# First feed-forward stage of an encoder layer: a second pair of features by seven products, plain blocks saved unscaled, and two steps exchanged

## The chip, the cores and the metric

The kernel runs on one core of a Trainium2 chip. A core has a matrix engine (TensorE; PE in the profile, its weight loads PEld), three engines for elementwise work (VectorE = DVE, ScalarE = ACT, GpSimd = POOL), a queue engine (SyncE = SP) and 16 DMA engines that bring data from device memory. The metric is the device time of one execution in microseconds, lower is better. The time before is 1250.46 us, the median of three runs that lie between 1250.18 and 1250.67.

## What is computed

One encoder layer on 512 tokens of width 1024: a half-step gated feed-forward network, a mixer of two attention branches, a second half-step feed-forward network, a final norm. The change lies in the two feed-forward stages, which are the same computation with different weights:

```python
def rmsnorm(x, g):
    y = xf * lax.rsqrt(jnp.mean(xf * xf, axis=-1, keepdims=True) + EPS)
    return (y * g.astype(jnp.float32)).astype(x.dtype)

def swiglu(x, w1, w3, w2):
    return (jax.nn.silu(x @ w1) * (x @ w3)) @ w2
...
x = x + 0.5 * swiglu(rmsnorm(x, ffn1_norm[l]), ffn1_w1[l], ffn1_w3[l], ffn1_w2[l])
h = rmsnorm(x, mix_norm[l])
x = x + hybrid_mixer(h, ...)
x = x + 0.5 * swiglu(rmsnorm(x, ffn2_norm[l]), ffn2_w1[l], ffn2_w3[l], ffn2_w2[l])
return rmsnorm(x, final_norm)
```

The hidden width is 2816, which the kernel treats as 22 features of 128 rows each; a feature needs one block of w1 and one of w3 (each 128 columns of weights over K = 1024, 512 KB).

## The kernel before

Activations are held transposed: model dimension on the partitions (eight tiles of 128), the 512 tokens along the free axis. Every float32 product is made of three passes on TensorE: operands are split into a high part H (a rounded copy, made by ACT) and a low part L (the remainder, made by DVE), and `mm3` (L256) adds H·H, H·L and L·H into one PSUM bank.

**Weights.** `self.order` lists all weight blocks of the program in the order of use; `loads` (L192) issues their DMAs as soon as a raw buffer is free, `prep` (L228) splits a raw block into `wh` and `wl` (lines L243 on ACT and L244 on DVE), `weights` (L248) hands the next one to TensorE. Split blocks have three buffers `wh` and one more, `whx`, for every fourth; raw blocks lie in rings `wr`, `wa`, `ws`, `wt`. `turn_of` (L122) orders the DMAs. TensorE's instructions keep the order in which the program writes them. The order on the other engines and on the queues is set ahead of time by a planner, which takes instructions in program order where it can and lets a later one go first when the earlier is not ready by its own estimate. Each queue then works strictly in its order.

**Plain features.** `feat` (L268) multiplies one block of 128 features with all 512 tokens: eight k-tiles of three matmuls of 512 columns, 24 matmuls for a block and 96 for two features. The first two blocks of the program are woven by `pair` (L278), since they run while x still arrives. `done1` and `done3` (L488 to L495) scale a block by `R`, the inverse root mean square of each token, apply SiLU, multiply, and split the result (`keep`). R itself comes from the squares of x (`norm_sq`, L402, hooked at step 12), their column sums on TensorE (`stat_r`, L419, hooked at 23), a power on POOL (L417), and four transposes on TensorE with a copy by ACT (`stat_R`, L428, hooked at 28). Until R is there the first blocks are held in their PSUM banks (the list `held`).

**Pairs by seven products.** The other features go two at a time through `strassen` (L310): seven steps A11, S1, S2, A12, S3, S4, A22 in place of eight, each one weight block of 24 matmuls of 256 columns. A11, A12 and A22 use quarters of the weights as they are; S1 and S3 are sums of two quarters, of which the first is loaded by SP (L224) and the second added onto it by an accumulating DMA of POOL (L225); S2 and S4 are sums made by DVE (L242). The steps S1, S2 and A22 multiply sums of activations, `TH` and `TL`, which `t_steps` (L341) prepares: eight scaled copies by ACT (L353), sums by DVE (L366, L367), splits (L358, L359), and for S3 and S4 new right halves of `hH` and `hL` (`part1`, L361, which may be written only when the plain blocks are done). The products of one pair collect in three PSUM banks: A11, S2, S3 and A22 in one after another ("A"), S1 and S4 in "Y", A12 in "X"; `evict` (L504) takes out the bank after each step. `slots` (L131) interleaves pairs so that steps of different pairs alternate; with `ahead`, used for the first group of stage "b" alone, its first five steps are A11 and A12 of the first pair, A11 of the second, S1 and S2 of the first.

**Stages.** `GROUPS` (L22) gives the plain features and the ends of the groups: in the first feed-forward stage ("a") features 0 to 3 are plain and 4 to 7 make two pairs of the first group, in the second ("b") there are no plain ones. After a group, `blocks` multiplies its features with w2 and adds the result to x.

## Time and profile before

| what | value |
|---|---|
| median of three runs | 1250.46 us |
| time of the profiled execution | 1250.19 us |
| its span in the profile | 1248.4 us |
| granted TensorE clock over the span | 0.998 |
| TensorE busy | 1234.5 us |
| DVE busy | 908.1 us |
| ACT busy | 603.5 us |
| POOL busy | 126.5 us |

The profiled execution ends 1.8 us after its span and lies 0.27 us under the median. A timeline row gives start and duration in us, the engine, the line of the kernel, the operation, and what it writes and reads; in brackets stands the idle time of the engine ahead of it and what ended it. Matmuls are pipelined, so that the distance from one start to the next, not the duration, tells their pace.

### The profile page before, as it was taken

Reading aid. Unit: us, or ns where it says so; the run is one execution under the profiler, and the core shown is the slowest. Engines: PE = TensorE matmul, PEld = TensorE weight load, DVE = VectorE, ACT = ScalarE, POOL = GpSimd, SP = SyncE. Lnnn points to the kernel's source line nnn. Section 1 sums busy time; section 2 is a strip of 40 time slices with the busy share of each in tenths; the row PEclk is TensorE's granted clock in tenths of the full one; section 3 lists DMA queues with packets and bytes.
Section 4 is the critical chain, followed back from the end, with each engine's and each line's share of the span. In section 5 each row is a group of like instructions: output and inputs, shape, how many; then the busy total and the mean of one; then the engine's idle time right before and its main releaser. Section 6 shows DMA issues by size and latency. Waiting matters only on the chain.

```text
span 1248.4 us, 20502 instructions
## 1 busy us (share of the span) xinstructions
PE 1234.5 (99%) x8220; PEld 1115.5 (89%) x8220; DVE 908.1 (73%) x1373; ACT 603.5 (48%) x897; POOL 126.5 (10%) x132
## 2 busy tenths in 40 slices
PE   9999999999999999999999999999999999999997
PEld 7897999899899999978888878888899989988997
DVE  7784688468787887477755898865978747874874
ACT  8551355245464444454423446654565425532553
POOL 1111101000222110200000200000211001100001
PEclk9999999999999999999999999999999999999999
DMA  8875777241488982653343131167767536743222
GB/s 296 230 192 166 195 196 192 95 119 51 143 214 252 233 223 105 226 170 79 94 132 101 51 110 43 66 217 246 205 169 193 163 101 185 187 152 104 66 85 68
DMA packets 90656, 190.85 MB, mean 153 GB/s; under 512 B 12849, under 2 KB 19393, under 8 KB 90561
## 3 DMA queue, kind: packets, MB, share of 16 engines
q1 hardware_dynamic: 71344, 145.46, 34.8%
q0 software_dynamic: 18496, 43.54, 17.4%
q8 instruction: 64, 1.05, 0.4%
q10 hardware_dynamic: 720, 0.55, 0.1%
q14 instruction: 32, 0.25, 0.1%
HBM read 175.79 MB, written 17.38 MB: 155 GB/s over the span
## 4 chain that ended last, share of the span: by engine, by line
PE 94%; DVE 3%; issue 1%; ACT 1%; POOL 0%; DMA 0%; SPq 0%; POOLq 0%; DVEq 0%
PE mm L258 24%; PE mm L260 23%; PE mm L259 23%; PE Y L260 4%; PE Y L259 4%; PE Y L258 4%; PE X L259 2%; PE X L260 2%; PE X L258 2%; PE mm L979 1%; PE S L903 1%; PE Tb L1115 1%; PE T L990 1%; DVE wl L244 0%; PE Sb L260 0%
## 5 line engine op out<-in xcount | busy, mean ns | idle before, releaser
L243 ACT CAST wh<-wr 128x1024 fp32r<-128x1024 f32 x133 | 139.4, 1049 | 188.0 <-PE mm L259 124.0
L244 DVE TENSOR_TENSOR wl<-wr,wh 128x1024 fp32r<-128x1024 f32 x133 | 163.1, 1226 | 55.4 <-ACT wh L243 55.2
L258 PE MATMUL mm<-hH,wh 128*128 128x256 f32 (+1 forms) x560 | 179.8, 321 | 1.7 <-ACT c L514 1.5
L260 PE MATMUL mm<-hH,wl 128*128 128x256 f32 (+1 forms) x560 | 177.2, 316 | 0.9 <-DVE wl L244 0.9
L259 PE MATMUL mm<-hL,wh 128*128 128x256 f32 (+1 forms) x560 | 177.3, 317 | 0.2 <-DVE hL L400 0.2
L258 PE MATMUL mm<-gg,wh 128*128 128x512 f32 (+1 forms) x440 | 166.4, 378 | 0.0
L259 PE MATMUL mm<-gg,wh 128*128 128x512 f32 (+1 forms) x440 | 165.9, 377 | 0.0
L260 PE MATMUL mm<-gg,wl 128*128 128x512 f32 (+1 forms) x440 | 165.9, 377 | 0.0
L258 PEld LDWEIGHTS mm<-hH,wh 128*128 128x128 f32 x560 | 105.4, 188 | 11.0 <-ACT c L514 1.7
L260 PEld LDWEIGHTS mm<-hH,wl 128*128 128x128 f32 x560 | 105.3, 188 | 9.1 <-DVE wl L244 1.3
L259 PEld LDWEIGHTS mm<-hL,wh 128*128 128x128 f32 x560 | 105.5, 188 | 8.3 <-DVE hL L400 1.2
L243 ACT CAST wh<-wa 128x1024 fp32r<-128x1024 f32 x54 | 56.8, 1051 | 97.0 <-PE Y L259 47.1
L258 PEld LDWEIGHTS mm<-gg,wh 128*128 128x128 f32 x440 | 82.6, 188 | 16.6 <-PE mm L260 0.9
L260 PEld LDWEIGHTS mm<-gg,wl 128*128 128x128 f32 x440 | 82.6, 188 | 15.4
L259 PEld LDWEIGHTS mm<-gg,wh 128*128 128x128 f32 x440 | 82.6, 188 | 14.9
L243 ACT CAST wh<-ws 128x1024 fp32r<-128x1024 f32 x54 | 56.8, 1052 | 72.9 <-PE mm L259 51.4
L243 ACT CAST wh<-wt 128x1024 fp32r<-128x1024 f32 x54 | 56.8, 1052 | 67.7 <-PE mm L259 44.0
L258 PE MATMUL mm<-TH,wh 128*128 128x256 f32 x320 | 88.4, 276 | 0.0
L260 PE MATMUL mm<-TH,wl 128*128 128x256 f32 x320 | 88.3, 276 | 0.0
L259 PE MATMUL mm<-TL,wh 128*128 128x256 f32 x320 | 88.3, 276 | 0.0
L244 DVE TENSOR_TENSOR wl<-wt,wh 128x1024 fp32r<-128x1024 f32 x54 | 66.0, 1223 | 30.7 <-ACT wh L243 29.9
L244 DVE TENSOR_TENSOR wl<-wa,wh 128x1024 fp32r<-128x1024 f32 x54 | 66.0, 1221 | 25.2 <-ACT wh L243 25.1
(275 smaller groups left out, 3200.5 us busy)
## 6 DMA issues: line engine op xcount, KB each, us to landing
wr<-in_w2a SPq DMA_DIRECT2D x22, 512.0 KB, 3.3
wt<-in_w13b SPq DMA_DIRECT2D x22, 512.0 KB, 4.2
wa<-in_w13b SPq DMA_DIRECT2D x22, 512.0 KB, 3.6
wt<-in_w13b POOLq DMA_DIRECT2D x22, 512.0 KB, 5.9
wr<-in_w2b SPq DMA_DIRECT2D x22, 512.0 KB, 3.6
wt<-in_w13a SPq DMA_DIRECT2D x18, 512.0 KB, 3.4
wt<-in_w13a POOLq DMA_DIRECT2D x18, 512.0 KB, 6.3
wa<-in_w13a SPq DMA_DIRECT2D x18, 512.0 KB, 3.3
```

The source lines that it names most:

```text
L243: self.nc.scalar.copy(H, raw)
L244: self.nc.vector.tensor_sub(L, raw, f32(H))
L258: mm(out, lH, rH, start=start, stop=False, skip_group_check=more)
L259: mm(out, lH, rL, start=False, stop=False, skip_group_check=more)
L260: mm(out, lL, rH, start=False, stop=stop, skip_group_check=more)
L903: nc.tensor.matmul(*args, start=True, stop=True)
L979: nc.tensor.matmul(oc, v, p, start=st, stop=sp)
L990: nc.tensor.transpose(ps[:, 128 * b:128 * b + 128], P[h][:, c0 + 128 * b:c0 + 128 * b + 128], self.ident)
L1115: nc.tensor.transpose(pt[:, 128 * j:128 * j + 128], P[h, j][:, 128 * k:128 * k + 128], self.ident)
```

## The change

In the first feed-forward stage two features are plain instead of four, and the first group has three pairs instead of two. The four plain blocks are copied out of PSUM by ACT as they are (`save`), and scaled, passed through SiLU, multiplied and split from there (`finish`) after the sixth and the seventh step of the pairs. `stat_r` and `stat_R` move behind the third and the fifth step of the pairs, the squares to step 24 of the plain part, and the preparation of the activation sums starts at step 13 and goes on at every step, with the sum for A22 left for the third step of the pairs. The accumulating DMAs are put into a list, `sums`; those of the first group of stage "a" are written into the program when at most five blocks lie between the block and the one in use. The first loads of the sums in that group have a turn that is one later. `slots` with `ahead` is used for the first group of both stages, and its sixth and seventh step (S3 of the first pair, S1 of the second) change places. Everything behind the first group keeps its form; the indices of the weight blocks behind it grow by three, since eight plain blocks become four and fourteen steps become twenty-one.

```diff
@@ -19,7 +19,8 @@
 BUFS = {"wr": 3, "wa": 3, "ws": 2, "wt": 4, "wh": 3, "whx": 1}
 BASE = {"wh": 160, "whx": 32}
 EARLY, EARLIER = 4, 6
-GROUPS = {"a": (4, 8, 16, 22), "b": (0, 8, 16, 22)}
+NEAR = 5
+GROUPS = {"a": (2, 8, 16, 22), "b": (0, 8, 16, 22)}
 PAIRS = ((0, 0), (1, 0), (0, 1), (0, 2), (1, 1), (1, 2), (2, 0), (3, 0), (2, 1), (2, 2), (3, 1), (3, 2))
 NSQ, FG, FV = 10, 10, 12
 HEAD_G = 4
@@ -112,6 +113,7 @@
             self.order += [(name, m * n + i) for i in range(m)]
         self.order += [(name, i) for name in ("wpb", "wo") for i in range(8)]
         self.order += self.ffn_order("b")
+        self.sums = []
         self.raws, self.tiles, self.used, self.wx, self.TQ, self.stage = {}, [], 0, None, None, None
         self.cap = len(self.order)
         self.rings = {k: [] for k in BUFS}
@@ -125,21 +127,21 @@
         s, f = self.order[n][0][2], self.order[n][1][0]
         if s == "q":
             return max(n - EARLY, self.index["swq", (0, "A11")] - 1)
-        return n - (EARLIER if f >= GROUPS[s][1] else EARLY)
+        return n - (EARLIER if f >= GROUPS[s][1] else EARLY - (s == "a"))
 
     @staticmethod
     def slots(fs, ahead=False):
         at = {7 * i + 2 * j: (f, step) for i, f in enumerate(fs) for j, step in enumerate(STEPS)}
         order = [at[k] for k in sorted(at)]
         if ahead:
-            order[:5] = [order[n] for n in (0, 3, 4, 1, 2)]
+            order[:7] = [order[n] for n in (0, 3, 4, 1, 2, 6, 5)]
         return order
 
     def ffn_order(self, s):
         first, *ends = GROUPS[s]
         items, lo, n = [("w13" + s, i) for i in range(2 * first)], first, 0
         for hi in ends:
-            items += [("sw" + s, at) for at in self.slots(range(lo, hi, 2), not lo)]
+            items += [("sw" + s, at) for at in self.slots(range(lo, hi, 2), lo == first)]
             nf = hi - (0 if n == 0 else lo)
             items += [("w2" + s, n + i) for i in range(nf)]
             n, lo = n + nf, hi
@@ -192,6 +194,8 @@
     def loads(self):
         while self.todo and self.load(self.todo[0]):
             self.todo.pop(0)
+        while self.sums and (not self.sums[0][1] or self.sums[0][0] - self.used <= NEAR):
+            self.sums.pop(0)[2]()
 
     def load(self, n):
         tag = self.kind[n]
@@ -222,7 +226,8 @@
             nc.sync.dma_start(dst, part(step))
         elif tag == "wt":
             nc.sync.dma_start(dst, part("A21"))
-            nc.gpsimd.dma_start(dst, part("A22" if step == "S1" else "A11"), accum_op=ALU.add)
+            self.sums.append((n, name == "sw" + "a" and f < GROUPS["a"][1],
+                              lambda: nc.gpsimd.dma_start(dst, part("A22" if step == "S1" else "A11"), accum_op=ALU.add)))
         return True
 
     def prep(self):
@@ -308,7 +313,7 @@
                     yield from part(c, j)
 
     def strassen(self, s, fs, evict):
-        st, order = {}, self.slots(fs, s == "b" and not fs[0])
+        st, order = {}, self.slots(fs, s != "q" and fs[0] == GROUPS[s][0])
         end = self.used + len(order) - 1
         for f, step in order:
             self.cap = end if f == fs[-1] and step in ("A12", "S3") else len(self.order)
@@ -366,8 +371,8 @@
         sub = lambda o, a, b: nc.vector.tensor_sub(raw[o], raw[a], raw[b])
         neg = lambda o, a, b: nc.vector.scalar_tensor_tensor(raw[o], raw[a], -1.0, raw[b], op0=ALU.mult, op1=ALU.subtract)
         return ([lambda d=d: put(d) for d in range(NK)]
-                + [lambda: sub(0, 0, 1), lambda: sub(1, 3, 1), lambda: neg(3, 3, 0), lambda: part(0),
-                   lambda: neg(2, 3, 2), lambda: part(3), lambda: part(2)], [lambda k=k: part1(k) for k in range(4)])
+                + [lambda: sub(0, 0, 1), lambda: part(0), lambda: sub(1, 3, 1), lambda: neg(3, 3, 0), lambda: part(3)],
+                [lambda k=k: part1(k) for k in range(4)] + [lambda: neg(2, 3, 2), lambda: part(2)])
 
     def block(self, name, n):
         if n % 8 == 0:
@@ -458,11 +463,11 @@
             self.gp = [gp] * 4
 
     def gtile(self, n, dtype=F32R):
-        return self.gp[n].tile([128, 2048], dtype, tag=f"g{n}", name="gg" if dtype == F32R else f"T{n - 2}")
+        return self.gp[n].tile([128, 2048], dtype, tag=f"g{n}", name="gg" if dtype == F32R else "T" if n > 1 else "uv")
 
     def ffn_run(self, s, gin, gnext, hooks, out=None, side={}):
         nc = self.nc
-        g, t, c, half = [], {}, {}, []
+        g, c, half = [], {}, []
 
         def new():
             both = self.gtile(len(g) // 2)
@@ -485,14 +490,18 @@
             nc.vector.tensor_sub(turn(L), src, turn(f32(H)))
             g.extend((H[:, T * j:T * j + T], L[:, T * j:T * j + T]) for j in range(2))
 
-        def done1(ps):
-            t[1] = self.tmp.tile([128, T], F32, tag="t", name="t1")
-            nc.vector.tensor_mul(t[1], ps, self.R)
-            nc.scalar.activation(t[1], t[1], AF.Silu)
-
-        def done3(ps):
-            nc.vector.scalar_tensor_tensor(t[1], ps, -1.0, t[1], op0=ALU.mult, op1=ALU.mult)
-            keep(t[1])
+        first, *ends = GROUPS[s]
+        plain = self.gtile(1, F32) if first else None
+
+        def save(i):
+            return lambda ps: nc.scalar.copy(plain[:, T * i:T * i + T], ps)
+
+        def finish(f):
+            u, v = (plain[:, T * i:T * i + T] for i in (2 * f, 2 * f + 1))
+            nc.vector.tensor_mul(u, u, self.R)
+            nc.scalar.activation(u, u, AF.Silu)
+            nc.vector.scalar_tensor_tensor(v, v, -1.0, u, op0=ALU.mult, op1=ALU.mult)
+            keep(v)
 
         def folded(f):
             return out is not None and f >= ends[-2]
@@ -540,19 +549,10 @@
                     nc.vector.tensor_mul(hi, hi, c2)
                 keep2(c1)
 
-        held = []
-
-        def later(fn):
-            return lambda ps: fn(ps) if held is None else held.append((fn, ps))
-
-        first, *ends = GROUPS[s]
-
-        def plain():
-            if s == "a":
-                yield from self.pair("w13a", (later(done1), later(done3)))
-            for f in range(s == "a", first):
-                yield from self.feat("w13" + s, 2 * f, later(done1))
-                yield from self.feat("w13" + s, 2 * f + 1, later(done3))
+        def head():
+            yield from self.pair("w13a", (save(0), save(1)))
+            for i in (2, 3):
+                yield from self.feat("w13a", i, save(i))
 
         def add(x, ps, R):
             if R is None:
@@ -572,18 +572,14 @@
                 nc.scalar.activation(self.x[d], self.x[d], AF.Copy, scale=self.par[:, gnext + d:gnext + d + 1])
 
         steps, late = self.t_steps(gin) if first else ([], [])
-        if not first:
-            held = None
-        for n, _ in enumerate(plain()):
+        for n, _ in enumerate(head() if first else ()):
             if n in hooks:
                 hooks[n]()
-                if hooks[n] == self.stat_R:
-                    for fn, ps in held:
-                        fn(ps)
-                    held = None
-            if n >= hooks["T"][0] and n % hooks["T"][1] == 0 and steps:
+            if n >= hooks["T"] and steps:
                 steps.pop(0)()
-        assert not steps and held is None
+        assert not steps
+        for f in range(first):
+            hooks["S"][5 + f] = lambda f=f: finish(f)
         lo, n = first, 0
         for gi, hi in enumerate(ends):
             last = hi == NF
@@ -591,8 +587,8 @@
                 for fn in late[:2]:
                     fn()
                 del late[:2]
-                if not lo and n1 in hooks:
-                    hooks[n1]()
+                if lo == first and n1 in hooks["S"]:
+                    hooks["S"][n1]()
 
             def done(d, ps, gi=gi, last=last):
                 down(d, ps, last)
@@ -1258,7 +1254,7 @@
                 self.norm_sq(d, 0)
 
         with tc.tile_pool(name="bt", bufs=1, side="right") as bp:
-            hooks = {12: squares, 23: self.stat_r, 28: self.stat_R, "T": (16, 2)}
+            hooks = {24: squares, "T": 13, "S": {2: self.stat_r, 4: self.stat_R}}
             self.bias_open(bp)
             side = {(0, d): lambda g=d: self.bias_rows(g) for d in range(3)}
             for h in range(8):
@@ -1269,7 +1265,7 @@
                 self.wx = None
         self.fctx = ExitStack()
         self.mixer()
-        self.ffn_run("b", G_FFN2, G_FIN, {3: self.stat_r, 5: self.stat_R}, out)
+        self.ffn_run("b", G_FFN2, G_FIN, {"S": {3: self.stat_r, 5: self.stat_R}}, out)
         self.wx = None
         self.fctx.close()
         self.hctx.close()
```

## The prediction, made before the changed kernel was seen

> **What bounds the kernel now.** The page first: its span, the busy times, and the chain that ended last.
>
> ```profile
> span 1248.4 us, 20502 instructions
> PE 1234.5 (99%) x8220; PEld 1115.5 (89%) x8220; DVE 908.1 (73%) x1373; ACT 603.5 (48%) x897; POOL 126.5 (10%) x132
> ...
> PE 94%; DVE 3%; issue 1%; ACT 1%; POOL 0%; DMA 0%; SPq 0%; POOLq 0%; DVEq 0%
> ```
>
> TensorE carries 94% of the chain. Time is won by taking matmuls out or by closing a gap of TensorE, and nowhere else. So I went on to the order of time, TensorE alone, through the two places that the change touches. The plain blocks first:
>
> ```profile
> 17.32 0.39 PE L260 MATMUL mm<-hH,wl 128*128 128x512 f32 x1
> ...
> 19.48 0.50 PE L260 MATMUL mm<-hH,wl 128*128 128x512 f32 x1 [0.88 <-DVE wl L244]
> ...
> 24.60 0.95 PE L424 MATMUL stat<-ones,acc 128*128 128x1 f32 x8
> 25.41 0.48 PE L258 MATMUL mm<-hH,wh 128*128 128x512 f32 x1
> ...
> 28.90 0.60 PE L433 MATMUL rb<-ident,r 128*128 128x128 f32 x4
> 29.25 0.48 PE L258 MATMUL mm<-hH,wh 128*128 128x512 f32 x1
> ...
> 30.50 0.39 PE L260 MATMUL mm<-hH,wl 128*128 128x512 f32 x1
> ...
> 52.94 0.39 PE L260 MATMUL mm<-hH,wl 128*128 128x512 f32 x1
> 53.16 0.28 PE L258 MATMUL mm<-hH,wh 128*128 128x256 f32 x1
> ```
>
> From 30.50 to 52.94 lie 99 matmuls of 512 columns, 0.2267 us apart, without a gap: a plain block of 24 takes 5.44 us. The third block of the program (the first of `feat`) begins with a hole: its second weight half comes at 19.48 instead of 17.55 + 2 × 0.227 = 18.00, so 1.48 us are lost. The statistics take 25.41 − 24.60 = 0.81 and 29.25 − 28.90 = 0.35 us of TensorE's stream. The steps of the pairs follow, by stretches (columns: stretch, length, then busy time of PE, PEld, DVE, ACT and POOL with counts, granted clock, DMA share, GB/s):
>
> ```profile
> 20.00:53.16 33.16, 33.16 (x153) 27.57 (x153) 27.66 (x33) 20.42 (x28) 5.60 (x4) 1.00 0.99 301
> ...
> 53.16:55.99 2.83, 2.83 (x26) 2.82 (x24) 2.40 (x3) 1.57 (x2) 1.15 (x1) 1.00 0.02 6
> 55.99:91.37 35.38, 35.38 (x315) 35.38 (x313) 28.45 (x29) 19.02 (x22) 3.65 (x4) 1.00 0.75 195
> sum 38.21, PE 38.21 PEld 38.20 DVE 30.86 ACT 20.59 POOL 4.80; mean PE 19.11 PEld 19.10 DVE 15.43 ACT 10.29 POOL 2.40
> ```
>
> 53.16 to 91.37 are the 14 steps of two pairs. The first takes 2.83 us, the other thirteen 35.38 / 13 = 2.72. DVE works 30.86 us there, 15.4 for a pair. DMA is full up to 53 us and no longer behind it.
>
> **The exchange of two features.** Removed: four plain blocks, 4 × 5.44 = 21.76 us. Added: seven steps, 7 × 2.72 = 19.05. That is **−2.7 us**, and TensorE's own, so no other engine hides it. Statistics cost the same 0.81 and 0.35 behind the third and fifth step.
>
> But steps at the start of a stage can be slower. Stage "b" already runs in the order that "a" now takes, with the statistics among its steps:
>
> ```profile
> 904.42 0.28 PE L258 MATMUL mm<-hH,wh 128*128 128x256 f32 x1
> ...
> 915.84 0.95 PE L424 MATMUL stat<-ones,acc 128*128 128x1 f32 x8
> 916.64 0.37 PE L258 MATMUL mm<-TH,wh 128*128 128x256 f32 x1
> ...
> 919.43 0.28 PE L260 MATMUL mm<-TH,wl 128*128 128x256 f32 x1
> ...
> 924.08 0.60 PE L433 MATMUL rb<-ident,r 128*128 128x128 f32 x4
> 924.43 0.36 PE L258 MATMUL Y<-TH,wh 128*128 128x256 f32 x1
> ...
> 930.07 0.28 PE L258 MATMUL mm<-TH,wh 128*128 128x256 f32 x1
> ...
> 919.63 1.04 ACT L243 CAST wh<-ws 128x1024 fp32r<-128x1024 f32 x1 [2.19 <-PE mm L259]
> 920.58 0.58 ACT L514 COPY c<-mm 128x512 f32<-128x512 f32 x1
> 921.22 0.39 PE L258 MATMUL mm<-hH,wh 128*128 128x256 f32 x1 [1.50 <-ACT c L514]
> ```
>
> 904.42 to 930.07 are eight steps in 25.65 us; less the statistics (0.80 and 0.35) and the wait at 921.22 (1.79 − 0.11 = 1.68) they are 22.82, or 2.85 a step. If "a" starts like that it pays 8 × 0.13 = 1.07, of which 0.11 is paid already in its first step: between 0 and 0.95. I take **+0.6**, nearer to that row since the order will be the same.
>
> The Trainium skill speaks against the exchange here. "TensorE: Matmul & The Clock Gate", section "Back-to-back issue gap", says that matmul spacing in a real stream is set by weight load and matmul together, 81 ns at 128 columns and 131 ns at 512. By an estimate between them, 98 ns at 256, a pair would cost 168 × 0.098 = 16.5 us against 96 × 0.131 = 12.6, and the exchange would lose 3.9. The trace disagrees: weight loads are busy without a break (35.38 of 35.38) and the spacing is still half that of 512 columns.
>
> **The two exchanged steps in the second stage.** The 1.68 us gap at 921.22 stands before S3 of the first pair. S2, just ended, and S3 use the same bank; ACT must copy it out first (0.58 us, L514), and that copy stands behind a cast of 1.04. With S1 of the second pair between them (2.72 us or more) the copy is done by 921.2 and S3 is due after 922.2. What is late next would be that S1. Its weights are the last `wl<-wt` before the gap:
>
> ```profile
> 915.07 1.22 DVE L244 TENSOR_TENSOR wl<-wt,wh 128x1024 fp32r<-128x1024 f32 x1
> ...
> 917.07 2.03 POOL L417 TENSOR_TENSOR r<-ms,mhalf 128x4 f32<-128x4 f32 x1 [5.11 <-DVE ms L416]
> ```
>
> They are ready at 916.3, due at 919.5; its bank "Y" is another; the power is done at 919.1, before the transposes that follow that step at 922.3. So **−1.6**, between −1.7 and 0. Behind it TensorE runs on to the end of the stage, so the gain stays.
>
> **The third block's hole.** Who held DVE and ACT ahead of 18.21?
>
> ```profile
> 15.22 1.66 ACT L408 ACTIVATE sq<-x 128x512 f32<-128x512 f32 x3
> 16.79 1.03 ACT L243 CAST wh<-wr 128x1024 fp32r<-128x1024 f32 x1
> ...
> 16.02 2.28 DVE L410 TENSOR_TENSOR acc<-acc,sq 128x512 f32<-128x512 f32 x3
> 18.21 1.22 DVE L244 TENSOR_TENSOR wl<-wr,wh 128x1024 fp32r<-128x1024 f32 x1
> ```
>
> Squares, though they are written behind many of the others. They move from step 12 to 24, but the activation sums come up to step 13, so the planner has something else to put there. From −1.48 (no hole) to +1.2 (a 1.2 us sum in front as well): I take **−0.7**.
>
> **DVE's queue.** This is the cover that could go. Up to 91.37 DVE works 27.66 + 30.86 = 58.5 of 71.4 us from 20 us on. The added pair brings 15.4; the two plain features take away four `wl` (1.22) and six operations on 512 columns (0.69), 9.0; `finish` keeps its operations, from SBUF. So 64.9 of 71.4 − 2.7 − 0.7 = 68.0, 95%. If all seven additions of squares (0.68 each, 4.8) come after 20 us and nothing of the sums goes ahead in exchange, 69.7 of 68.0: 1.7 late, and with the waits of a strict queue some 3. TensorE has split weights for about three steps ahead, so single delays are hidden: between 0 and +3, I take **+0.5**, by the rows at 53 to 91, where DVE waits for ACT and TensorE and not the other way.
>
> **Other additions.** ACT gets four copies of 0.58 and three more casts of 1.05: 5.5 us more on an engine busy 20.42 of 33.16. SP gets three more loads, POOL two more accumulating ones of 1.2 us; I cost both at nothing, as DMA has room behind 53 us, and take the case where it has not as a rival. The later accumulation takes pressure off the front; nothing there waits for it now.
>
> **Sum:** −2.7 + 0.6 − 0.7 + 0.5 − 1.6 = −3.9. The profiled execution took 1250.19 (span 1248.4 and 1.8 around it), so 1246.3; the median lies 0.27 higher: **1246.6 us**. With every term at its low end it is 5.9 less than now, 1244.6; with the pace and the third block's hole at their high ends 1.7 less, 1248.8, which is the forecast's own range. DVE's high end is a rival of its own; all high ends together, with nothing won in the second stage, would be 2.5 slower.
>
> **Rivals.**
>
> *DVE's queue becomes the bound of the first group.* All 3 us are lost there, a gain of 1.4 is left: 1249. For it stands the 95%; against it, that DVE waits in the present pairs. Chance 0.13.
>
> *The fourth block's load comes late.* Its raw buffer is that of the first block; loads without such a wait may pass it on SP.
>
> ```profile
> 10.79 0.42 SPq L209 DMA_DIRECT2D wr<-in_w13a  x1
> 11.36 0.38 SPq L224 DMA_DIRECT2D wt<-in_w13a  x1
> 15.02 4.76 SPq L209 DMA_DIRECT2D wr<-in_w13a  x3
> ...
> 25.37 1.05 ACT L243 CAST wh<-wr 128x1024 fp32r<-128x1024 f32 x1 [0.41 <-DMA wr<-in_w13a]
> ```
>
> One does already (11.36 ahead of 15.02). Now up to seven are ready there (three quarters A, four first halves of sums). Each is 0.52 MB, 1.7 us at the 301 GB/s above. Three in front move that block from landing before 20 us to about 24, its split to 26.5, due at 23.5 to 24: 3 us of stall, 1249.6. Against it: only one passed. Chance 0.10.
>
> *R comes late and the kernel is slower.* The transposes behind the fifth step are due at 29.3 + 5 × 2.85 + 0.8 = 44.4; sums of columns at 37.9, DVE and POOL's power (2 us) give about 41.2: 3.2 us to spare. POOL works in order, and an accumulating DMA set before the power waits for its first half:
>
> ```profile
> POOL wt L225 <- DMA wt<-in_w13a: 45.4, 8, 16.8
> ```
>
> Eight such waits, 5.7 us each, the longest 16.8. A wait of w stalls TensorE for w − 3.2; slower than before it becomes from w = 7.1, beyond 0.2% from 9.6. At 16.8: 13.6 − 3.9 = 9.7 slower, 1260. Against it: these waits are mostly of an idle POOL, and late writing puts later halves behind the power. Chance 0.07.
>
> *Weight loads pace all steps,* 2.85 for 21 of them: 59.9 us against 57.1, the exchange is worth nothing, 1248.8 with the rest. The thirteen steps at 2.72 speak against it. Chance 0.02.
>
> *A different plan of the mixer,* since block indices move by three: 3 us either way. TensorE's stream leaves little to win there. Chance 0.06.
>
> **How the numbers follow.** Forecast 0.62. About 0.2% (2.5 us) is what a measurement of this kernel can tell from no change. That bound lies at 1248.0, inside the forecast's range, of whose 0.62 some 0.05 lies above it. Faster by that: 0.57 and half of the last case, 0.60; slower: late R and part of the last, 0.09; within: the others, 0.31. The range runs from a little under the forecast's low end, for a better plan of the mixer, to above the two rivals that eat most of the gain: 1244.0 to 1250.4.
>
> **What would show it.** Right: step distance 2.72 to 2.85 from about 30 us, the first w2 product near 89, no gap before S3 of stage "b", the third block's second half before 19 us. Wrong: TensorE waiting for `wl` of DVE between 30 and 89 (the queue), for `wh` of the fourth block near 24 (the load), at the transposes behind the fifth step (R), or a gap before S1 of the second pair of "b".

## The result and the profile after

The changed kernel takes 1254.6 us (median of 14 runs, 1252.35 to 1259.1) against 1250.68 (14 runs of the kernel before on the same chip, 1250.17 to 1251.28). The ratio is 1.0036, with a 95% interval from 1.0028 to 1.0044: slower by 4 us, where 4 us less had been forecast. The kernel before scatters by 1.1 us, the changed one by 6.8. Both halves of that sentence need a cause.

The profiled execution is the fastest of the fourteen, 1252.35 us with a span of 1250.6. Its page, the span, the busy times and the shares of the chain:

```profile
span 1250.6 us, 20659 instructions
...
PE 1233.6 (99%) x8292; PEld 1117.1 (89%) x8292; DVE 913.4 (73%) x1379; ACT 609.4 (49%) x905; POOL 129.0 (10%) x134
...
PE 90%; DVE 4%; DMA 3%; ACT 1%; issue 1%; POOL 1%; SPq 0%; POOLq 0%; DVEq 0%
```

TensorE is busy 0.9 us less than before, and the span is 2.2 us longer. DMA, which had no share of the chain, now has 3%: TensorE waits for something that comes from memory. To find where, I take marks in TensorE's order of time: the first matmul of the pairs, the first w2 product of the first group, the column sums before the mixer and in the second stage, the first transposes of the mixer, and the last column sums. Before (the two marks that the prediction shows are 53.16 and 915.84):

```profile
91.37 0.39 PE L258 MATMUL mm<-gg,wh 128*128 128x512 f32 x1
...
352.75 0.39 PE L424 MATMUL stat<-ones,acc 128*128 128x1 f32 x3
...
545.86 0.41 PE L990 MATMUL T<-ident,P 128*128 128x128 f32 x2 [0.53 <-DVE MX L911]
...
1231.29 0.28 PE L424 MATMUL stat<-ones,acc 128*128 128x1 f32 x2
```

After, with the waits of the first group in their places:

```profile
30.05 0.28 PE L263 MATMUL mm<-hH,wh 128*128 128x256 f32 x1
...
35.73 0.28 PE L264 MATMUL mm<-hL,wh 128*128 128x256 f32 x1
37.68 0.38 PE L265 MATMUL mm<-hH,wl 128*128 128x256 f32 x1 [1.68 <-DVE wl L249]
...
46.71 0.28 PE L265 MATMUL mm<-TH,wl 128*128 128x256 f32 x1
47.47 0.65 PE L438 MATMUL rb<-ident,r 128*128 128x128 f32 x4 [0.48 <-POOL r L422]
...
91.69 0.39 PE L263 MATMUL mm<-gg,wh 128*128 128x512 f32 x1
...
353.32 0.28 PE L429 MATMUL stat<-ones,acc 128*128 128x1 f32 x2
...
548.76 0.41 PE L986 MATMUL T<-ident,P 128*128 128x128 f32 x2 [1.23 <-DVE MX L907]
...
918.85 0.94 PE L429 MATMUL stat<-ones,acc 128*128 128x1 f32 x8
...
1232.76 0.39 PE L429 MATMUL stat<-ones,acc 128*128 128x1 f32 x3
```

| mark | before | after | longer in the stretch that ends there |
|---|---|---|---|
| first w2 product | 91.37 | 91.69 | +0.3 |
| column sums before the mixer | 352.75 | 353.32 | +0.3 |
| first transposes of the mixer | 545.86 | 548.76 | +2.3 |
| column sums of the second stage | 915.84 | 918.85 | +0.1 |
| last column sums | 1231.29 | 1232.76 | −1.5 |
| end of the span | 1248.4 | 1250.6 | +0.7 |

The last row is not part of the argument: over the fourteen profiles of this study the time from the last column sums to the end of the span lies between 17.1 and 17.8 us, and what moves it stays open.

The reader is to see three things. The second stage gives its 1.5 us. The first group, which should have ended 2.3 us earlier (2.7 − 0.6 + 0.7 − 0.5), ends 0.3 later: from 30.05 to 91.69 are 61.64 us, of which 21 × 2.72 + 0.81 + 0.35 = 58.3 are work at the pace of before. Of the other 3.4 us, 1.95 − 0.11 = 1.84 stand before the first `wl` of the third step, 0.76 − 0.11 = 0.65 before the transposes of R, and 0.9 are the slower pace of the first steps. And the mixer's entry costs 2.3 us more.

Who was late for the third step? ACT, DVE and POOL of the changed kernel at that time, one fence for each:

```profile
31.19 1.05 ACT L248 CAST wh<-wt 128x1024 fp32r<-128x1024 f32 x1 [3.60 <-DMA wt<-in_w13a]
...
33.81 1.03 ACT L248 CAST wh<-wa 128x1024 fp32r<-128x1024 f32 x1
```

```profile
31.19 1.23 DVE L247 TENSOR_TENSOR ws<-wt,wa 128x1024 f32<-128x1024 f32 x1 [3.69 <-DMA wt<-in_w13a]
...
36.41 1.22 DVE L249 TENSOR_TENSOR wl<-wa,wh 128x1024 fp32r<-128x1024 f32 x1
```

```profile
20.69 1.36 POOL L230 DMA_DIRECT2D wt<-in_w13a  x1 [19.43 <-DMA wt<-in_w13a]
...
44.88 1.20 POOL L230 DMA_DIRECT2D wt<-in_w13a  x1 [8.47 <-DMA wt<-in_w13a]
45.72 1.70 POOL L422 TENSOR_TENSOR r<-ms,mhalf 128x4 f32<-128x4 f32 x1
```

The first sum is whole when its accumulating load, issued at 20.69, has landed at 31.2, 10.5 us later. ACT and DVE stand idle for it, 3.60 and 3.69 us, since ACT's cast of that sum, and on DVE the addition that makes the next sum from it, come first in their order. The cast and the `wl` of the third step, whose weights are plain and long there, are queued behind them. And POOL starts the power for R only when the fifth accumulating load is out, which waited 8.47 us for its first half: R's operand `ms` was ready at 44.25, the power starts at 45.72.

### The profile page after: what moved, and what is told of

Read it like the earlier page. It is cut to its first block, busy times and chain, and to the rows that moved or that the text cites. A ratio compares the mean times of both kernels' runs of the same rounds, so it can differ in the third digit from the quotient of the medians.

```text
span 1250.6 us, 20659 instructions
## 1 busy us (share of the span) xinstructions
PE 1233.6 (99%) x8292; PEld 1117.1 (89%) x8292; DVE 913.4 (73%) x1379; ACT 609.4 (49%) x905; POOL 129.0 (10%) x134
## 3 DMA queue, kind: packets, MB, share of 16 engines
q8 instruction: 65, 1.06, 0.3%
## 4 chain that ended last, share of the span: by engine, by line
PE 90%; DVE 4%; DMA 3%; ACT 1%; issue 1%; POOL 1%; SPq 0%; POOLq 0%; DVEq 0%
PE mm L263 22%; PE mm L264 22%; PE mm L265 22%; PE Y L264 4%; PE Y L263 4%; PE Y L265 4%; PE X L264 2%; PE X L265 2%; PE X L263 2%; DMA wt<-in_w13a 2%; PE S L899 1%; PE mm L975 1%; PE Tb L1111 1%; PE T L986 1%; DMA wt<-in_waq 1%
## 5 line engine op out<-in xcount | busy, mean ns | idle before, releaser
L249 DVE TENSOR_TENSOR wl<-wr,wh 128x1024 fp32r<-128x1024 f32 x130 | 159.3, 1225 | 54.0 <-ACT wh L248 53.6
L263 PE MATMUL mm<-hH,wh 128*128 128x256 f32 (+1 forms) x544 | 171.1, 315 | 0.4 <-ACT hH L404 0.4
L265 PE MATMUL mm<-hH,wl 128*128 128x256 f32 (+1 forms) x544 | 169.2, 311 | 2.3 <-DVE wl L249 2.3
L264 PE MATMUL mm<-hL,wh 128*128 128x256 f32 (+1 forms) x544 | 169.2, 311 | 0.4 <-DVE hL L405 0.3
L265 PEld LDWEIGHTS mm<-hH,wl 128*128 128x128 f32 x544 | 102.1, 188 | 9.6 <-DVE wl L249 2.9
L263 PEld LDWEIGHTS mm<-hH,wh 128*128 128x128 f32 x544 | 102.3, 188 | 8.4 <-issue 1.0
L264 PEld LDWEIGHTS mm<-hL,wh 128*128 128x128 f32 x544 | 102.2, 188 | 7.8 <-DVE hL L405 1.9
L263 PE MATMUL mm<-TH,wh 128*128 128x256 f32 x336 | 92.9, 276 | 0.0
L264 PE MATMUL mm<-TL,wh 128*128 128x256 f32 x336 | 92.8, 276 | 0.0
L265 PE MATMUL mm<-TH,wl 128*128 128x256 f32 x336 | 92.8, 276 | 0.0
```

The source lines that it names most:

```text
L249: self.nc.vector.tensor_sub(L, raw, f32(H))
L263: mm(out, lH, rH, start=start, stop=False, skip_group_check=more)
L264: mm(out, lH, rL, start=False, stop=False, skip_group_check=more)
L265: mm(out, lL, rH, start=False, stop=stop, skip_group_check=more)
```

## The experiments

Twelve runs were made; they are told here in the order of the argument. In the diffs the lines are those of the kernel from which each starts. Each ran beside the kernel before on the same chip.

**1. The two exchanged steps alone**, in the kernel before:

```diff
-            order[:5] = [order[n] for n in (0, 3, 4, 1, 2)]
+            order[:7] = [order[n] for n in (0, 3, 4, 1, 2, 6, 5)]
```

> The kernel before, with only the sixth and seventh step of the second stage exchanged. Theory (the second stage did what was forecast, and the loss lies in front of it): the 1.7 us gap of TensorE before S3 of the first pair goes, nothing else changes: 1249.1 us, ratio 0.9987. Rival (the exchange only moves the gap, and the 1.5 us that the changed kernel won back behind 919 us have another source): 1250.6 us.

Measured: 1248.86 us (median of 11 runs; one of them at 1264.09) against 1250.52, ratio 0.9998 with an interval of 0.9977 to 1.0018 that this one run makes wide. So it was run again:

> The kernel before the change with the exchange of the two steps in the second stage alone, once more, since one run of eleven stood 13 us above the others. Theory: 1.5 to 1.7 us under the kernel before, ratio 0.9987 with an interval below 1. Rival, the gap only moves: ratio 0.9995 to 1.0005.

Measured: 1248.45 us (1248.12 to 1248.88, 11 runs) against 1250.57, ratio 0.9981 (0.9972 to 0.9989). The gap of 1.68 us before S3 is gone, and nothing took its place. This one line is the fastest version of the study, faster than both kernels.

**2. The first group without its accumulating loads**, in the changed kernel (what S1 and S3 then multiply is one quarter, and the output is wrong):

```diff
-        while self.sums and (not self.sums[0][1] or self.sums[0][0] - self.used <= NEAR):
-            self.sums.pop(0)[2]()
+        while self.sums:
+            n, first, fn = self.sums.pop(0)
+            if not first:
+                fn()
```

> The changed kernel with the six accumulating loads of the first group left out, so S1 and S3 of its three pairs hold one quarter of the weights instead of the sum of two. Theory (in the first group DVE, ACT and POOL stand behind loads that come later than planned): no instruction waits 3.7 us for such a load, TensorE's waits of 1.7 us (for the split weights of the third A step) and 0.5 us (for R) go, and the scatter between executions with them: 1252.0 us or less, within 1 us from lowest to highest. Rival (DVE's work alone fills the first group): DVE has the same work, so the times stay at 1252.4 to 1259.

Measured: 1250.03 us (1249.17 to 1253.98, 11 runs), ratio 0.9997 (0.9989 to 1.0006). TensorE no longer waits between the pairs, and the first w2 product comes at 88.98. DVE does as much as in the changed kernel or more (columns as in the prediction's table of stretches), first the changed kernel, then this one:

```profile
20.00:91.40 71.40, 69.25 (x560) 67.09 (x559) 65.30 (x73) 45.31 (x61) 13.57 (x11) 1.00 0.91 249
```

```profile
20.00:91.40 71.40, 71.40 (x573) 69.19 (x572) 67.82 (x76) 47.41 (x62) 8.05 (x5) 1.00 0.72 215
```

67.82 us of DVE's work fit into 71.4 without a wait of TensorE. So the amount of DVE's work is not the bound; the loads of the sums are what makes the first group late, and the DMA share falls from 0.91 to 0.72 with them. Two things did not come as expected. The scatter did not fall under 1 us: it is 4.8 us, and 2.1 without the slowest run. And the kernel as a whole is only as fast as before, though its first group ends 2.4 us earlier: from the column sums to the mixer's first transposes it takes 545.73 − 350.60 = 195.1 us (before 193.1), and from there to the column sums of the second stage 371.2 (before 370.0; 370.9 in the first profile of experiment 1, where nothing ahead of the second stage was changed). So the loads of the first group are not the whole loss.

**3. Bytes, or the addition in the DMA engines?** The second half of each sum of the first group is loaded over the first in place of being added to it:

```diff
-    lambda: nc.gpsimd.dma_start(dst, part("A22" if step == "S1" else "A11"), accum_op=ALU.add)))
+    lambda: nc.gpsimd.dma_start(dst, part("A22" if step == "S1" else "A11"),
+                                **({} if name == "swa" and f < GROUPS["a"][1] else {"accum_op": ALU.add}))))
```

> The changed kernel in which the second half of each sum of the first group of stage a is loaded over the first half in place of being added to it: the same bytes, the same queue of POOL, the same buffers and waits, but no addition in the DMA; S1 and S3 hold one quarter, so the output differs. Theory A, the addition in the DMA engines is the cost: in the kernel before, 4.16 MB of the accumulating queue took 34.3% of the engines' time between 20 and 91.4 us and 12.63 MB of the other queue 48.4%, that is 8.2% and 3.8% for a MB; without the addition the DMA share falls from 0.91 to about 0.8, the waits of the first group mostly go, 1250.5 (the run without these loads gave 1250.0). Theory B, bytes and the chain of two loads one after the other with a buffer held meanwhile are the cost: the waits stay, 1252.4 to 1254.6 as the changed kernel.

Measured: 1251.98 us (1249.84 to 1255.28, 11 runs) against 1250.63, ratio 1.0006 (0.9997 to 1.0016); the changed kernel itself, on the same chip, is in experiment 8 with 1255.12 and a ratio of 1.0031. The DMA queues between 20 and 91.4 us (columns: packets, MB, share of the 16 engines), the changed kernel and then this one:

```profile
q1 hardware_dynamic: 5984, 12.45, 49.8%
q0 software_dynamic: 2720, 5.24, 41.2%
```

```profile
q1 hardware_dynamic: 6168, 13.05, 52.2%
q0 software_dynamic: 1952, 5.24, 31.1%
```

The same 5.24 MB of the accumulating queue take 41.2% of the engines' time with the addition and 31.1% without it (the later group's loads still add); a MB of the plain queue takes 4.0%, one of this queue 7.9% and 5.9%. The wait for the third step falls to 0.2 us, that for R stays at 0.7 us, and the first w2 product comes at 90.14 us. Both theories have a part: by the ratios (1.0031 with the addition, 1.0006 without it, 0.9997 without the loads) most of what these loads cost goes with the addition. That some stays is seen in the profile, 90.14 against 88.98; the intervals of the last two ratios overlap.

**4. The index alone put back.** In the changed kernel, the blocks behind the first group take buffers by their old indices:

```diff
+    def phase(self, n):
+        return n - 3 if n >= self.index["w2a", 0] else n
...
-            return 160 - 128 * (n % 2)
+            return 160 - 128 * (self.phase(n) % 2)
...
-        tag = "whx" if ... and n % 4 == 3 and ...
+        tag = "whx" if ... and self.phase(n) % 4 == 3 and ...
```

> The changed kernel, where the weight blocks behind the first group take the extra split buffer and the addresses by their old indices (three less). Theory (the 2.3 us between 353 and 549 us come from the shift of the indices: the last w2 block is split early, a load that waits for its raw buffer stands ahead of the sums' loads on SP): the stretch from the column sums at 353 us to the transposes at 549 us is as long as before, and the time is 2.3 us less than the changed kernel's beside it. Rival (that stretch is longer because of timing that the first group leaves behind): no gain.

Measured: 1251.42 us (1249.29 to 1254.05, 11 runs), ratio 1.0007 (0.9998 to 1.0016). From the column sums to the first transposes it takes 546.33 − 352.56 = 193.8 us, where before took 193.1 and the changed kernel 195.4; 1.7 of the 2.3 us are back. By the ratios (1.0036 and 1.0007) the old indices are worth more, 3.6 us; where the rest comes from is not located, since the first group takes 61.4 us in this profile and 61.6 in the changed kernel's. The order of SP shows how, first the changed kernel, then this one:

```profile
339.10 6.55 SPq L226 DMA_DIRECT2D wr<-in_waq  x2
347.87 0.37 SPq L228 DMA_DIRECT2D wt<-in_waq  x1
```

```profile
338.35 0.38 SPq L229 DMA_DIRECT2D wr<-in_waq  x1
341.67 0.38 SPq L231 DMA_DIRECT2D wt<-in_waq  x1
```

With the new indices SP meets a load of `wr` whose buffer is still in use and stands before it until 345.6; the first loads of the mixer's sums queue behind, 6 us later than here.

**5. The index alone shifted**, in the kernel before (the same lines with `n + 3`):

> The kernel before the change, but the weight blocks behind the first group take buffers as if their indices were three higher, which is all that the change does behind that group in the first stage and the mixer. Theory: the stretch from the column sums before the mixer (352.75) to the first transposes (545.86) grows from 193.1 to about 195, 1252.2 us. Rival: the longer stretch comes from what the first group leaves behind (landing times, the state of the buffers), not from the indices: 1250.5.

Measured: 1251.97 us (1251.28 to 1252.93, 11 runs) against 1250.63, ratio 1.0009 (1.0000 to 1.0018). Its profile shows SP's long stand as in the changed kernel, but the stretch is 545.86 − 352.83 = 193.0 us, not 195: the late loads were just in time there. So the time came out near the theory and its place did not. The two medians say that the shift of the index costs something, with an interval that just reaches 1. Its place is not found: the profile's 0.9 us lie between the transposes and the second stage (370.9 for 370.0 us), and the first profile of experiment 1 has the same 370.9 without the shift. That the index alone makes the 2.3 us is not shown, and what else enters stays open.

**6. The order of ACT, DVE and POOL put right by hand.** The cast of the first sum behind that of the third step, the next sum's addition behind that step's `wl`, and POOL's accumulating loads from the fifth on behind the power:

```diff
+            with self.tc.issue_after(self.pow.ins) if first and n >= 17 else ExitStack():
+                fn()
...
+            with self.tc.issue_after(self.low.ins) if n == 8 else ExitStack():
+                self.nc.vector.tensor_add(raw, a, b)
+        with self.tc.issue_after(self.high.ins) if n == 7 else ExitStack():
+            high = self.nc.scalar.copy(H, raw)
...
```

> The changed kernel with three orders pinned: the cast of S1 of the first pair behind that of the third A step on ACT, the addition for S2 behind the third A step's low part on DVE, and the fifth accumulating load behind the power for R on POOL. Theory (it is the order in the strict queues that hands the late loads on to TensorE): the waits of 1.7 and 0.5 us go, 2.3 us less than the changed kernel, and less scatter: about 1252. Rival (DVE's work fills the group, whatever its order): the waits move to other steps and the time stays.

Measured: 1254.32 us (1251.89 to 1257.82, 8 runs), ratio 1.0028 (1.0015 to 1.0040). Both waits of the first group are gone, and a new one of 2.0 us stands at 58 us, where DVE waited 4.95 us for the next accumulating load; from 30.05 to the first w2 product it is 61.4 us, as in the changed kernel. A single wait was not the loss: the loads were late, and whichever step met them first paid.

**7. The turn of the first sum put back**, in the kernel of experiment 4:

```diff
-        return n - (EARLIER if f >= GROUPS[s][1] else EARLY - (s == "a"))
+        return n - (EARLIER if f >= GROUPS[s][1] else EARLY)
```

> The changed kernel with the block indices behind the first group as before (as in the run with the phase alone, 1251.4 us), and in addition the first loads of the sums of stage a's first group take the turn that they had before: the quarter A21 of the first sum is issued ahead of the third quarter A. Theory, supply: the accumulating load that makes the first sum whole lands some 5 us earlier than at 31.2 us, so the cast of that sum no longer holds the third step; the wait of 1.8 us at 37 us goes, and with it some of what follows: 1249.3 to 1250.2. Rival, the order of the loads is worth nothing because the DMA engines are full: the wait only moves to a later step, the first group ends at the same time, 1251.4. Second rival: the fourth plain block comes late behind one more load in front of it, 1252 or more.

Measured: 1254.76 us (1253.24 to 1257.27, 6 runs) against 1250.63, ratio 1.0031 (1.0020 to 1.0043): slower than experiment 4. The time is that of the second rival, the mechanism is not: the fourth block is in time, and the third step no longer waits either. But TensorE waits 2.99 us for R, and the profile shows something new behind that wait, in stretches of 2 us (the last three columns are the granted clock, the DMA share and GB/s):

```profile
46.00:48.00 2.00, 0.27 (x3) 0.27 (x3) 1.97 (x2) 0.00 (x0) 1.68 (x1) 1.00 0.62 203
48.00:50.00 2.00, 2.00 (x13) 2.00 (x12) 0.73 (x2) 1.53 (x2) 0.23 (x1) 0.58 1.10 225
50.00:52.00 2.00, 2.00 (x13) 2.00 (x12) 1.25 (x2) 1.92 (x3) 1.01 (x1) 0.57 1.07 329
```

For some 4 us the clock that TensorE was granted is little over one half.

**8. The changed kernel again**, to see whether this happens to it too:

> The changed kernel once more, beside the others on this chip. The supply theory says that its scatter (1252.35 to 1259.1 us) comes from the landing times of the accumulating loads in the first group, so a profile with a higher time shows longer waits there and the same time elsewhere. The rival (the mixer's part) says that the stretch from 353 to 549 us varies.

Measured: 1255.12 us (1252.32 to 1256.94, 6 runs) against 1250.63, ratio 1.0031 (1.0019 to 1.0043). The profiled run took 1253.55. TensorE at the third step:

```profile
35.71 0.28 PE L264 MATMUL mm<-hL,wh 128*128 128x256 f32 x1
38.16 0.39 PE L265 MATMUL mm<-hH,wl 128*128 128x256 f32 x1 [2.17 <-DVE wl L249]
...
38.73 0.31 PE L263 MATMUL mm<-hH,wh 128*128 128x256 f32 x1
38.85 0.41 PE L264 MATMUL mm<-hL,wh 128*128 128x256 f32 x1
39.06 0.42 PE L265 MATMUL mm<-hH,wl 128*128 128x256 f32 x1
```

The wait is 2.34 us, half a us longer than in the first profile, and behind it the matmuls start 0.213 us apart in place of 0.113; by the stretches the clock is 0.71 from 38 to 40, 0.50 from 40 to 42, 0.94 from 42 to 44, a loss of 2 × (0.29 + 0.50 + 0.06) = 1.7 us. The first profile, with a wait of 1.84, shows 1.00 throughout. From the first w2 product to the column sums both profiles take 261.6 us; the mixer's entry is 0.6 us longer in this one. The mean clock over the span follows the times: the fourteen runs of the changed kernel stand at 0.997 or 0.998 for 1252.4 us and at 0.992 for 1258.65 and 1259.1. A thousandth of 1250 us is 1.25 us, so by an estimate from these numbers the 0.005 between them are some 6 us of the 6.5.

**9. Work put into the wait.** Ten matmuls of no use ahead of the third step of the changed kernel, so that the wait cannot be 2 us long:

```diff
+            if s == "a" and fs[0] == GROUPS[s][0] and (f, step) == order[2]:
+                for _ in range(10):
+                    self.nc.tensor.matmul(ps[:, :256], self.hH[0][:, :128], self.hH[0][:, :256], start=True, stop=True)
```

> The changed kernel with ten matmuls of 256 columns that compute nothing of use (their bank is started anew by the step) ahead of the third step of the pairs, where TensorE waits 1.84 us in the profile at 1252.35 us and 2.34 us in that at 1253.55 us. Theory, the clock: behind an idle stretch of TensorE of over 2 us the granted clock falls to 0.5 to 0.7 for some 3.5 us (0.71, 0.50 and 0.94 in the stretches from 38 to 44 us of the second profile, none under 1.00 in the first), which costs some 1.7 us more and happens in most of the runs whose mean clock is 0.996 or less; with 10 x 0.113 us of work in the wait the idle stretch stays under 1.3 us, the mean clock is 0.997 or 0.998 in all runs, the median falls to 1252.3 to 1253 and no run is over 1254.5. Rival, the scatter has another source: the median stays at 1254.6 to 1255.1 and runs up to 1257 remain.

Measured: 1256.23 us (1254.65 to 1259.38, 5 runs), ratio 1.0047 (1.0034 to 1.0060). A miss: that wait falls to 0.5 us, but now TensorE waits 3.01 us for R, and the clock falls behind that (0.81, 0.50 and 0.84 from 48 to 54 us). The test of the clock failed by a second late thing, and it raised the question why R, a power of four columns, can be so late.

**10. The turn, and the power ahead of the fifth accumulating load**, in the kernel of experiment 7, which has the old indices and the old turn:

```diff
+            n, first, fn = self.sums.pop(0)
+            with self.tc.issue_after(self.pow.ins) if first and n >= 17 else ExitStack():
+                fn()
```

> The changed kernel with three of its parts put back: the block indices behind the first group as before, the turn of the first loads of the sums as before, and POOL's power for R ahead of the fifth accumulating load (behind it the power ended 2.8 us late in the run with the turn, at 47.7 us). Theory, the waits and the clock are the whole loss of the first group: without the wait for the third step, without that for R and without the clock's fall behind it the first w2 product comes at about 89 us in place of 91.4 before, the mixer's entry costs 0.7 us more than before and the second stage 1.6 less: 1247.0 to 1248.6. Rival, supply by the DMA engines: the wait moves to a sum further on (as it did to 58 us when the order alone was changed), first w2 product at 91 us or later, 1250.5 or more.

Measured: 1254.33 us (1248.43 to 1256.40, 12 runs) against 1250.57, ratio 1.0025 (1.0014 to 1.0035). One run of twelve shows the first theory's time; the others have the rival's time, but not its place. POOL and then DVE of the profiled run:

```profile
43.31 6.49 POOL L427 TENSOR_TENSOR r<-ms,mhalf 128x4 f32<-128x4 f32 x1 [10.22 <-DMA wt<-in_w13a]
```

```profile
43.08 0.15 DVE L426 TENSOR_SCALAR ms<-stat 128x4 f32<-128x4 f32 x1
43.15 1.21 DVE L252 TENSOR_TENSOR ws<-ws,wa 128x1024 f32<-128x1024 f32 x1
44.28 1.22 DVE L254 TENSOR_TENSOR wl<-wt,wh 128x1024 fp32r<-128x1024 f32 x1
45.42 1.22 DVE L369 TENSOR_TENSOR TL<-T,TH 128x1024 fp32r<-128x1024 f32 x1
46.55 1.22 DVE L254 TENSOR_TENSOR wl<-ws,wh 128x1024 fp32r<-128x1024 f32 x1
47.69 1.22 DVE L252 TENSOR_TENSOR ws<-wt,wa 128x1024 f32<-128x1024 f32 x1
48.94 1.22 DVE L252 TENSOR_TENSOR ws<-ws,wa 128x1024 f32<-128x1024 f32 x1
```

No load stands before the power on POOL any more (the DMA in its row landed at 43.27, when the operand was ready too, at 43.23), and it takes 6.49 us. Look at where DVE's operations meet: 43.15 + 1.21 is 44.36, and the next starts at 44.28, before the end; so on until 47.69 + 1.22 = 48.91, then 48.94: the first gap, 0.03 us wide. The power ends at 49.80, 0.89 us behind it. In all nine profiles up to here with the changed first group the power ends 0.87 to 0.92 us behind the start of the first such gap.

**11. Operations of DVE that leave POOL's door open.** The same kernel, and four more operations like `ms`, which read four columns of PSUM, written behind it:

```diff
+        if self.used < 20:
+            spare = self.tmp.tile([128, 16], F32, tag="ms", name="spare")
+            for _ in range(4):
+                self.nc.vector.tensor_scalar(spare[:, :4], ps[:, s], 1.0 / D, EPS, op0=ALU.mult, op1=ALU.add)
```

> The kernel of the run with the turn and the power, and four operations of DVE more (the one that makes ms, written again to a tile that nobody reads: PSUM in, four columns) right behind ms. In that run the power took 6.49 us (43.31 to 49.80), TensorE waited 4.14 us and the clock fell. Theory, DVE keeps POOL out: in eight runs the power of the first group ended 0.86 to 0.92 us behind the first gap (0.03 us) between two operations of DVE with two SBUF inputs, whenever that came, so POOL's reading of SBUF waits as long as such operations follow each other without a gap; with operations that read PSUM alone the power goes in between: it takes 1.1 to 2.1 us, ends near 45 us, TensorE waits less than 1 us for it, the clock stays at 1.00, first w2 product at 89 to 90 us, time 1248.0 to 1250.0. Rival, the power is slow because POOL still writes the descriptors of the accumulating loads or because the DMA engines are full: it takes 3 to 6.5 us again and the time stays at 1254.

Measured: 1249.93 us (1249.42 to 1251.65, 11 runs) against 1250.80, ratio 0.9996 (0.9987 to 1.0005). DVE, where the planner put the four operations between the others, and then POOL:

```profile
43.24 0.15 DVE L440 TENSOR_SCALAR spare<-stat 128x4 f32<-128x4 f32 x1
43.31 1.21 DVE L252 TENSOR_TENSOR ws<-ws,wa 128x1024 f32<-128x1024 f32 x1
44.45 0.15 DVE L440 TENSOR_SCALAR spare<-stat 128x4 f32<-128x4 f32 x1
44.52 1.21 DVE L254 TENSOR_TENSOR wl<-wt,wh 128x1024 fp32r<-128x1024 f32 x1
```

```profile
43.41 2.02 POOL L427 TENSOR_TENSOR r<-ms,mhalf 128x4 f32<-128x4 f32 x1 [8.52 <-DVE spare L440]
```

The power takes 2.02 us and ends 1.0 us behind the start of the small operation at 44.45; TensorE does not wait for R at all; the clock stays at 1.00 through the group; the scatter falls from 8.0 us to 2.2 and the ratio from 1.0025 to 0.9996, with the DMA engines as full as before (0.92). So DVE kept POOL out, not the descriptors and not the DMA. The mark was missed, though: the first w2 product comes at 91.29 and not at 89 to 90, since 0.63 us are still waited at the third step and 1.13 at 87 us.

The next question is whether DVE also holds back the accumulating loads, which POOL issues. In the changed kernel the load issued at 20.69 landed after 10.5 us, with DVE busy 6.82 us of them and the DMA share at 1.06; the one issued at 83.79 landed after 6.6 us, with DVE busy 6.58 of them and the share at 0.76. So a busy DVE alone does not make a load late; the late one is the one that met full DMA engines.

Late writing of the accumulating loads (the list `sums` and `NEAR`) was not tried by itself, so no run shows what it does. Nor was the kernel of experiment 2 run with the old indices.

## Why the prediction was wrong

Step by step, by its own terms:

- **The exchange of two features, −2.7: the size was right, the stage could not feed it.** The pace of the later steps is 2.72 us, and without the sums' loads (experiment 2) the first w2 product comes at 88.98, as forecast ("near 89").
- **Slower steps at the start, +0.6:** 0.9 measured, inside the bounds that were given (0 to 0.95).
- **The third block's hole, −0.7:** the hole shrinks from 1.48 to about 0.8 us, but the pairs start only 0.2 us earlier than the four blocks would have let them (30.05 against 53.16 − 21.76 − 0.81 − 0.35 = 30.24), since the woven blocks ahead of it end 0.7 us later (last matmul at 18.04 for 17.32). A small miss.
- **The exchanged steps of the second stage, −1.6:** right, in place and size (−1.5; alone −2.1 between medians).
- **DVE's queue, +0.5, taken for a matter of the amount of work:** the amount did no harm (experiment 2). Its order did, by what DVE kept waiting: the splits behind a sum that had not landed, and POOL's power.
- **"Other additions … I cost both at nothing, as DMA has room behind 53 us": this step failed.** The pairs no longer began at 53 us but at 30, where the row of the prediction itself shows DMA full (0.99). Seven steps more ask for their halves in that time, a sum needs two loads one after the other into one of four `wt` buffers, and the second load of the first sum was 10.5 us on its way. In place of nothing this term cost 2.5 us of waits in the fastest run (1.84 for the third step, 0.65 for R), and with the loads left out both waits were gone (experiment 2). "TensorE has split weights for about three steps ahead, so single delays are hidden" was read from a stretch in which DMA was at 0.75 and did not hold at 0.91. Experiments 6, 7 and 9 show the wait moving as soon as one is closed.
- **R late, chance 0.07: the right place, and half of the reason.** In the changed kernel it was POOL's own queue, as the rival had it: the power stood 1.5 us behind the fifth load, and TensorE lost 0.65 us. But the margin of 3.2 us was built on a power of 2 us, from a row where DVE left a gap early. With DVE's queue packed the power took up to 6.49 us, and TensorE waited 3 to 4 us in experiments 7, 9 and 10. The rival did not look at DVE.
- **The mixer, 3 us either way, chance 0.06:** +2.3 came. In the six profiles with the changed first group and the new indices the stretch from the column sums to the transposes takes 195.1 to 196.2 us, in the four with the old indices 193.8 to 194.6, and in the four with the old first group 193.0 to 193.1, the shifted index of experiment 5 among them. So it takes both, the new indices and the changed first group; how the two work together stays open.
- **What was in no step:** TensorE was taken to lose only the length of a wait. Behind the longer waits the clock fell as well, for 1.7 us of loss each time. The mean clocks of the runs, and the scatter that goes in experiment 11, say that this makes most of the difference between the fastest run of the changed kernel, 1252.35, and its median, 1254.6; no run at the median was profiled, and the direct test, experiment 9, failed.

The failed step is not the whole distance of 8 us between forecast and result. No run has both the loads left out and the old indices, so whether 1246.6 could be reached with these two put right is not shown.

## What to carry to other kernels

A term that adds loads is priced in the stretch where these loads will run after the change, not where they run now; where DMA is full, find the first queue that stands in front of a load, and expect the wait to move, not to go, when the order is mended. A small operation of POOL that the critical path needs has no fixed price: look at what DVE runs beside it. And a long wait of TensorE can be paid twice: in the first group waits of up to 2.0 us cost their own length, those from 2.34 us on another 1.7 us.

## What the hardware showed that was not expected

**The clock behind a wait.** In the first group TensorE's starts lay 1.93, 1.95 and 2.10 us apart over three waits, and the clock stayed at 1.00; over 2.45, 3.10, 3.12 and 4.25 us the clock then fell to one half, each time for 3.41 us. While it was down, matmuls of 256 columns started 0.213 us apart in place of 0.113. In stretches of that length, the changed kernel's profile and then its second one (columns as above: length, busy time of PE, PEld, DVE, ACT, POOL, clock, DMA share, GB/s):

```profile
35.17:38.59 3.42, 1.74 (x16) 1.55 (x15) 3.42 (x6) 3.42 (x7) 1.20 (x1) 1.00 1.07 341
```

```profile
35.43:38.84 3.41, 1.24 (x10) 1.04 (x10) 3.41 (x5) 3.41 (x7) 0.78 (x1) 1.00 1.07 351
38.84:42.25 3.41, 3.41 (x18) 3.41 (x17) 3.41 (x7) 0.90 (x1) 0.00 (x0) 0.50 1.09 273
42.25:45.66 3.41, 3.41 (x31) 3.41 (x31) 3.41 (x5) 1.53 (x2) 0.97 (x2) 1.00 0.49 179
```

The fall does not come with the wait itself, but at times that keep a fixed distance: in the profile of experiment 7 the falls begin at 48.31 and 550.07, in that of experiment 10 at 49.81 and 551.58, in both 147 times 3.41 us apart. What counts is thus how busy TensorE was in one such stretch, and where a wait lies in it. In the stretch ahead of a fall in the first group it was busy 0.00 to 1.24 us of 3.41; 1.74 was enough to keep the clock. At the mixer's transposes, where short groups and waits alternate, the clock fell in four profiles for 3.41 us, once (experiment 4) behind a wait of only 1.4 us and a stretch with 1.89 us of small transposes, so busy time as the profile counts it is not the whole rule. The Trainium skill, "TensorE: Matmul & The Clock Gate", section "Part 1: The HAM clock gate", describes such a gate: half clock after an idle window of some 3.4 us that runs freely, full clock again after a busy one. The length of the slow stretch and the fixed distances agree with it. The trigger differs: the stretch ahead of a fall need not be idle, 2.45 us between two starts were enough.

**DVE can keep POOL out over several of its operations.** A power on 128 × 4 took 1.14 to 6.49 us, by what DVE ran beside it. The Trainium skill's page "SBUF — State Buffer", section "SBUF: two separate sides", says that an operation of DVE with two inputs in SBUF and a GpSimd operation that reads SBUF exclude each other, each for the whole instruction. The runs agree and add that one instruction's end can be too little: in experiment 10 five `tensor_tensor` in a row, each started before the last had ended, held POOL for 5.6 us, and in experiment 11 an operation with its input in PSUM let it in, in the other nine profiles of that first group a gap of 0.03 us. That is no general rule: in the kernel before a change from a `scalar_tensor_tensor` to a `tensor_tensor` at 26.8 us let the power in without a gap, and at the column sums before the mixer seven profiles show it going in between two `tensor_tensor` that overlap like the others (in the changed kernel at 357.5 us). What sets these apart is open.

**The accumulating queue** took 7.9% of the DMA engines' time for a MB in a window of 71.4 us, the plain queue 4.0%; where six of its ten loads did not add, 5.9%.
